# A two-layer attention encoder on one core: first weights through ScalarE's queue, norm factors beside x, and a first step ordered by product

## The chip, the core and the metric

The kernel runs on one core of one Trainium2 chip. The core has a matrix engine (TensorE, in the profile "PE" for its matmuls and "PEld" for its weight loads), three engines for elementwise work (VectorE "DVE", ScalarE "ACT", GpSimd "POOL") and a queue for transfers (SyncE, "SP"); ScalarE can issue transfers too ("ACTq" in the profile). Each engine works through its own list in order, and the lists are tied together by semaphores. Times are device microseconds of whole executions; the verdict rests on the median over runs. The measurement of the kernel before gave 853.75, 854.29 and 854.53 us, with a median of 854.29 us.

## The reference: what is computed

The input x has 512 tokens of 1024 values (float32). Two layers follow each other:

```
for i in range(DEPTH):                      # DEPTH = 2
    hn = rms_norm(x, norm_gain[i])
    if i % 2 == 0:  y = mixer_a(hn, ...)    # dilated windows, 3 groups, T5 bias
    else:           y = mixer_b(hn, ...)    # 2-D neighbourhood on an 8 x 64 grid
    x = x + y
```

Both mixers project hn with one wide weight matrix into queries, keys, values and a gate, norm queries and keys per head (with a gain per head dimension), add a learned bias to the scores, take a softmax, weigh the values, multiply by silu(gate) and project back to 1024. There are 16 heads of 64. In `rms_norm` each of the 1024 features has its factor in `norm_gain`; the division by the root of the mean square is per token.

## The kernel before

**Products in three parts.** Every float32 operand a is kept as a rounded part a_h (type float32r) and a rest a_l = a - a_h. A product is then three matmuls into one PSUM bank: a_h b_h, a_h b_l, a_l b_h (`mm3`). For weights, `split` makes the pair: ScalarE copies the raw weights to `wh` with rounding (L127), and VectorE or GpSimd subtracts (L131, `wl`; two of five go to GpSimd). For the normed input, `norm` makes `hn_h` on ScalarE (L379, x times the factor of its feature) and `hn_l` on VectorE (L380).

**Staging.** x lies transposed in SBUF as eight tiles of 128 features by 512 tokens (`x_all[:, k, :]`). Work goes over pairs of heads (hc, eight per layer). A projection (`project`) takes eight steps k, one per feature tile; in each step four token tiles i take three matmuls each, with `hn` as the stationary and `w` as the moving operand, into four PSUM accumulators. So a step has twelve matmuls. The division by the root of the mean square is applied later, when the accumulators are read, because the mean square of layer one is known only after all of x has been seen.

**Generators.** `loads`, `raws`, `splits` and `steps` (L157 to L196) hand the weights on in order. `raws` keeps three buffers `wraw` of 1024 columns in flight, each filled through SP's queue; the first is filled in two halves (L172 and L175), and one x load goes between them. `behind` holds three more x loads (tiles 2-3, 4-5, 6-7), one of which follows each later weights load. `splits` works up to four roundings ahead.

**What sets the order.** PE's order is written out by hand: `run` walks `main` (the projections) and lets `side` (norms, transposes, scores and so on) in between, by a planner's clock that adds a price per matmul. `project` yields after each token tile, and at each yield `pump` lets `side` go on when its due time is reached; `project` may also name a stamp that must be there first (`need`, here "na": norm k+1 must be written before step k of the first projection). The order on ACT, DVE, POOL and SP is laid out by the framework from a simulated timeline, except for instructions pinned with `keep_in_program_order`.

**The start.** SP loads x tile 0 (`load_x`, L343), the first half of the first weights (L172), x tile 1 and so on. ACT's queue loads `ng`, the 2 x 8 norm factors per partition (L349), and `hg`, the head gains (L363), from which four one-column VectorE instructions make `gk` (L366). Nine matmuls on a constant (`busy`, L358) keep PE occupied until data is there. `side` begins with the eight `norm` calls, each followed by the square of the tile before (L383, ScalarE) and later by the sums (L1146, VectorE).

Of the kernel before, what the change touches and what calls it, by code (L numbers as in the profile page):

```python
# [13 lines left out]
F32 = mybir.dt.float32  # L14
# [3 lines left out]
ALU = mybir.AluOpType  # L18
# [4 lines left out]
P = 128  # L23
S = 512
# [3 lines left out]
KT = 8  # L28
EPS = 1e-6
SCALE = DH ** -0.5  # L30
# [12 lines left out]
def tile_hybrid_encoder(  # L43
# [2 lines left out]
    xt: bass.AP,  # L46
    xg: bass.AP,
    w: bass.AP,
    norm_gain: bass.AP,
    head_gain: bass.AP,  # L50
    t5t: bass.AP,
    rpb: bass.AP,
# [4 lines left out]
    nc = tc.nc  # L57
# [3 lines left out]
    big = ctx.enter_context(tc.tile_pool(name="big", bufs=1))  # L61
# [21 lines left out]
    def bank(name):  # L83

        return ps_side.tile([P, 512], F32, tag="side", name=name)
# [13 lines left out]

    hn_h = big.tile([P, KT, S], F32R, name="hn_h")  # L100
    hn_l = big.tile([P, KT, S], F32R, name="hn_l")
    x_all = big.tile([P, KT, S], F32, tag="y", name="x_all")
    y_l = big.tile([P, KT, S], F32R, name="y_l")

    def rsqrt(eng, r, ss, n, scale):
# [16 lines left out]
    turn, pool = [0], [2, 5]  # L122

    def split(raw, n):
        h = wp.tile([P, 512], F32R, tag="wh", name="wh", bufs=4)[:, :n]
        l = wp.tile([P, 512], F32R, tag="wl", name="wl", bufs=4)[:, :n]
        nc.scalar.copy(h, raw)  # L127
        turn[0] += 1
        to_pool = turn[0] * pool[0] % pool[1] < pool[0]
        eng = nc.gpsimd if to_pool else nc.vector  # L130
        eng.tensor_sub(l, raw, h.bitcast(F32))  # L131
        return h, l
# [24 lines left out]
    def loads():  # L157
        for off, n, ks in blocks():
            per = 1024 // n
            for k in range(0, ks, per):  # L160
                m = min(per, ks - k)
                yield w[:, off + k * n : off + (k + m) * n], m * n, n
# [3 lines left out]
    def raws():  # L166
        queue = []
        for src, cols, n in loads():
            raw = wp.tile([P, 1024], F32, tag="wraw", name="wraw", bufs=3)
            dst = raw[:, :cols]  # L170
            if not begun:
                nc.sync.dma_start(dst[:, :n], src[:, :n])  # L172
                begun.append(load_x(1, 2))
                dst, src = dst[:, n:], src[:, n:]
            nc.sync.dma_start(dst, src)  # L175
            if behind:
                behind.pop()()
            queue.append((raw, cols, n))
            if len(queue) > 2:
                yield queue.pop(0)  # L180
        yield from queue
# [55 lines left out]
    def chore(now):  # L237

        if now and chores and next(chores[0], "end") == "end":
            chores.pop(0)  # L240

    def project(stat_h, stat_l, n, evac, guard, need=None):

        acc = {i: ps_acc.tile([P, 512], F32, tag="acc", name="acc") for i in range(4)}
        for k in range(KT):
            chore(1 <= k < KT - 2)
            if need:
                yield need, min(k + 1, KT - 1)
            if k == KT - 1:
                yield guard  # L250
            h, l = next(wsteps)
            for i in range(4):
                mm3(acc[i][:, :n], stat_h(k, i), stat_l(k, i), h, l, k == 0, k == KT - 1)
                if k == KT - 1:
                    evac(i, acc[i])
                yield
# [69 lines left out]
    ng = cp.tile([P, 2, KT], F32, name="ng")  # L326
# [13 lines left out]
        rsqrt(nc.vector, rs_n, ssq, 4, 1.0 / D)  # L340

    def load_x(k0, k1):
        nc.sync.dma_start(x_all[:, k0:k1, :], xt[:, k0:k1, :])  # L343

    warm = cp.tile([P, 1], F32, name="warm")
    nc.vector.memset(warm, 0.0)
    nc.scalar.activation(warm, warm, AF.Exp)
    load_x(0, 1)
    nc.scalar.dma_start(ng, norm_gain)  # L349
    behind += [  # L350
        lambda: load_x(6, KT),
        lambda: load_x(4, 6),
        lambda: load_x(2, 4),
    ]
    busy = bank("busy")
    for _ in range(9):
        wide = lambda n: ones[:, 0:1].to_broadcast([P, n])
        nc.tensor.matmul(busy, wide(P), wide(S), start=True, stop=True)  # L358
    wsteps = steps()
    wsteps = chain([next(wsteps)], wsteps)  # L360

    hg = cp.tile([P, 8], F32, name="hg")
    nc.scalar.dma_start(hg, head_gain)  # L363
    gk = cp.tile([P, 4], F32, name="gk")
    for i, (a, b) in enumerate(((0, 3), (1, 4), (2, 5), (6, 7))):
        nc.vector.scalar_tensor_tensor(  # L366
            gk[:, i : i + 1], hg[:, a : a + 1], -SCALE, hg[:, b : b + 1], op0=ALU.mult, op1=ALU.mult
        )

    def scales_a():  # L370
        pa = spread()
# [2 lines left out]

    def norm(layer, k, xk):

        g = ng[:, layer, k : k + 1]
        h, l = hn_h[:, k, :], hn_l[:, k, :]
        nc.scalar.activation(h, xk, AF.Copy, scale=g)  # L379
        return nc.vector.scalar_tensor_tensor(l, xk, g, h.bitcast(F32), op0=ALU.mult, op1=ALU.subtract)  # L380
# [755 lines left out]
    def side():  # L1136
        for k in range(KT):
            norm(0, k, x_all[:, k, :])
            if k:
                square_a(k - 1)  # L1140
            stamp["na", k] = 0
            yield 1000
        square_a(KT - 1)
        for k in range(1, KT):
            yield 1300
            nc.vector.tensor_add(x_all[:, 0, :], x_all[:, 0, :], x_all[:, k, :])  # L1146
        yield 1500
        row_scale(row_sums(x_all[:, 0, :]))
        st["y_h"] = big.tile([P, KT, S], F32R, tag="y", name="y_h")
        yield 2500  # L1150
        bias_lines()
        st["e", 0] = bias_a(0)
        yield 2500
        scales_a()
        first_out()
        stamp["rs", "a"] = 0
        for hc in range(NHC):
            if hc < NHC - 1:
                yield from k_a(hc)
                yield from chain(q_a(hc), v_a(hc))  # L1160
                if moved(hc):
                    yield from st.pop(("land", hc))
                yield from attn_a(hc)
                if hc == 1:
                    bias_rows()
            else:
                gap[0] = cycle((500, 500, 700))
                yield from chain(q_a(hc), k_a(hc))
                yield from attn_a(hc)
        yield from residual(xg)  # L1170
        stamp["ya", KT - 1, "y"] = 0
        yield "wait", ("x", KT - 1), 800
        for f in range(KT):
            square_b(f)
            yield 600
        yield 2600
        row_scale(row_sums(st.pop("ssq")))
        stamp["rs", "b"] = 0
        yield 5000
        nc.scalar.mul(rs_half, spread(), 0.5)  # L1180
        stamp["rs", "all"] = 0
        for hc in range(NHC):
            yield from side_b(hc)
        yield from residual(xm_d)
        stamp["yb", KT - 1, "y"] = 0

    run(main(), side())


# [27 lines left out]
def _layout(x, norm_gain, a_w_in, a_w_out, a_q_gain, a_k_gain, t5_bias,  # L1217
            b_w_in, b_w_out, b_q_gain, b_k_gain, b_rpb):
    f = lambda a: np.asarray(a)
    x, norm_gain, t5_bias = f(x), f(norm_gain), f(t5_bias)  # L1220
    wa, wao = f(a_w_in)[0].reshape(KT, P, -1), f(a_w_out)[0].reshape(KT, P, D)
    wb, wbo = f(b_w_in)[0].reshape(KT, P, -1), f(b_w_out)[0].reshape(KT, P, D)

    def outs(w):
        k = KT - 1
        blk = (w[:k, :, :512], w[:k, :, 512:896], w[k:, :, :512], w[k:, :, 512:896], w[:, :, 896:])
        return [b.transpose(1, 0, 2).reshape(P, -1) for b in blk]

    def cols(w, starts):
        blk = np.concatenate([w[:, :, s : s + P] for s in starts], axis=2)  # L1230
        return blk.transpose(1, 0, 2).reshape(P, -1)

    parts = []
    for hc in range(NHC):
        c = lambda g, i: (3 * g + i) * D + P * hc
        parts.append(cols(wa, [c(1, 1), c(2, 1), c(1, 2), c(2, 2)]))
        parts.append(cols(wa, [c(0, 0), c(1, 0), c(2, 0), c(0, 1)]))
        parts.append(cols(wa, [c(0, 2)]))
        parts.append(cols(wa, [9 * D + P * hc]))
    parts += outs(wao)  # L1240
    for hc in range(NHC):
        parts.append(cols(wb, [i * D + P * hc for i in range(3)]))
        parts.append(cols(wb, [3 * D + P * hc]))
    parts += outs(wbo)
    w = np.concatenate(parts, axis=1)

    hg = np.concatenate([f(a_q_gain)[0], f(a_k_gain)[0], f(b_q_gain), f(b_k_gain)]).T
    hg = np.concatenate([hg, hg])
    rt = f(b_rpb)[0].transpose(0, 2, 1)
    rpb = np.stack([rt[:, :, 7 - r + _GRID_ROWS] for r in _GRID_ROWS], axis=1).reshape(P, 248)  # L1250
    oh, mask = _constants()
    norm_gain = norm_gain.reshape(2, KT, P).transpose(2, 0, 1)
    xt = x[0].reshape(P, 4, KT, P).transpose(3, 2, 1, 0).reshape(P, KT, S)
    xg = x[0].reshape(8, 64, KT, P)[_GRID_ROWS].transpose(3, 2, 1, 0).reshape(P, KT, S)
    return [xt, xg, w, norm_gain, hg, t5_bias.T, rpb, oh, mask]


_NAMES = ["xt", "xg", "w", "norm_gain", "head_gain", "t5t", "rpb", "onehot", "maskc"]


# [17 lines left out]
```

## Time and profile before

| | |
|---|---|
| median of 3 runs | 854.29 us (853.75 to 854.53) |
| the profiled execution | 854.65 us, span 852.7 us |
| PE busy | 843.6 us (99% of the span), 5547 matmuls |
| PE weight loads busy | 702.7 us (82%) |
| DVE / ACT / POOL busy | 520.2 / 431.3 / 307.1 us |
| moved by the transfers | 141.23 MB, mean 166 GB/s |

The profiled execution lies 0.36 us above the median of the runs. Its span begins with the first instruction and ends with the last; 1.95 us of its time lie outside the span. The rows of a timeline give the start (us), the length (us), engine, line, operation, output and inputs; "xN" with a length covers N instructions that follow each other. In brackets stands how long the engine had been idle and what released it. PE's rows overlap: the distance between two starts tells the rate, not their lengths. The chain of waits follows the work that ended last back to its start, and prints it in order of time.

### The profile page before, as it was taken

How to read it: one execution, taken by the hardware profiler on the slowest of the kernel's cores; microseconds unless marked ns; L12 is line 12 of the kernel's file. 1: busy time of each engine (PE TensorE's matmuls, PEld its weight loads, DVE VectorE, ACT ScalarE, POOL GpSimd, SP SyncE). 2: the span in 40 equal slices, each digit the busy share in tenths (PEclk: the TensorE clock that was granted, in tenths of full speed). 3: DMA queues.
4: the chain of work that ended last, by engine and by line, in shares of the span. 5: the costliest groups of instructions: out<-in, count | busy, mean ns of one | idle time of the engine just before them, and what ended most of it. 6: DMA issues, size and time to landing. Idle time of an engine off the chain costs nothing.

```text
span 852.7 us, 15400 instructions
## 1 busy us (share of the span) xinstructions
PE 843.6 (99%) x5547; PEld 702.7 (82%) x5547; DVE 520.2 (61%) x1335; ACT 431.3 (51%) x924; POOL 307.1 (36%) x493
## 2 busy tenths in 40 slices
PE   8999999999999999999999999999999999999998
PEld 6788878788788788788788787789998898889786
DVE  6445684674675675675675745447567656766642
ACT  7433653653652652652653554355366655665531
POOL 2252541542542542542531341121344335542411
PEclk9999999999999999999999999999999999999999
DMA  7346277477478378378375562174245654555223
GB/s 250 111 130 208 87 226 219 153 222 227 137 230 241 105 239 240 98 238 238 96 247 153 147 190 78 60 244 142 82 142 150 168 162 149 170 163 160 99 98 126
DMA packets 65372, 141.23 MB, mean 166 GB/s; under 512 B 5904, under 2 KB 23248, under 8 KB 65296
## 3 DMA queue, kind: packets, MB, share of 16 engines
q1 hardware_dynamic: 65008, 140.24, 53.7%
q8 instruction: 44, 0.72, 0.4%
q14 instruction: 32, 0.26, 0.1%
q10 hardware_dynamic: 288, 0.01, 0.0%
HBM read 109.11 MB, written 31.12 MB: 164 GB/s over the span
## 4 chain that ended last, share of the span: by engine, by line
PE 87%; ACT 4%; DMA 4%; DVE 3%; issue 1%; POOL 1%; SPq 0%; ACTq 0%; POOLq 0%; DVEq 0%
PE acc L206 74%; PE log L206 5%; PE o L206 5%; PE tp L210 3%; DMA qd<-rawq 1%; ACT p L655 1%; ACT p L814 1%; DMA rp<-in_rpb 1%; ACT p L1067 1%; DMA qt<-qd 1%; POOL sq L270 1%; ACT wh L127 1%; DMA hg<-in_head_gain 0%; DVE wl L131 0%; DMA eb<-lb_d 0%
## 5 line engine op out<-in xcount | busy, mean ns | idle before, releaser
L127 ACT CAST wh<-wraw 128x512 fp32r<-128x512 f32 (+1 forms) x276 | 162.0, 588 | 291.4 <-PE acc L206 251.0
L206 PE MATMUL acc<-wh,hn_h 128*128 128x512 f32 (+1 forms) x768 | 294.2, 383 | 1.7 <-ACT wh L127 0.9
L206 PE MATMUL acc<-wh,hn_l 128*128 128x512 f32 (+1 forms) x768 | 286.3, 373 | 0.0
L206 PE MATMUL acc<-wl,hn_h 128*128 128x512 f32 (+1 forms) x768 | 285.8, 372 | 0.4 <-DVE wl L131 0.4
L131 POOL TENSOR_TENSOR wl<-wraw,wh 128x512 fp32r<-128x512 f32 (+1 forms) x110 | 137.0, 1245 | 359.4 <-ACT wh L127 320.0
L131 DVE TENSOR_TENSOR wl<-wraw,wh 128x512 fp32r<-128x512 f32 (+1 forms) x166 | 111.1, 670 | 135.8 <-ACT wh L127 131.5
L206 PEld LDWEIGHTS acc<-wh,hn_h 128*128 128x128 f32 x768 | 144.6, 188 | 29.3 <-issue 4.9
L206 PEld LDWEIGHTS acc<-wh,hn_l 128*128 128x128 f32 x768 | 144.4, 188 | 20.8
L206 PEld LDWEIGHTS acc<-wl,hn_h 128*128 128x128 f32 x768 | 144.8, 189 | 19.8 <-DVE wl L131 0.9
L206 PE MATMUL acc<-hn_h,wh 128*128 128x512 f32 x192 | 77.0, 401 | 0.9 <-ACT rawq L460 0.6
L206 PE MATMUL acc<-hn_h,wl 128*128 128x512 f32 x192 | 74.9, 390 | 0.0
L206 PE MATMUL acc<-hn_l,wh 128*128 128x512 f32 x192 | 74.8, 390 | 0.0
L655 ACT ACTIVATE p<-p,mn 128x512 f32<-128x512 f32 (+3 forms) x128 | 69.3, 586 | 0.0
L814 ACT ACTIVATE p<-p,mn 128x512 f32<-128x512 f32 (+1 forms) x64 | 44.8, 701 | 45.0 <-DVE mn L803 44.1
L273 DVE TENSOR_REDUCE ss<-sq 128x4 f32<-128x256 f32 (+1 forms) x96 | 48.4, 504 | 30.7 <-POOL sq L272 19.7
L727 DVE STREAM_TRANSPOSE tr<-p 128x512 f32<-128x512 f32 (+1 forms) x80 | 53.7, 682 | 9.9 <-ACT p L655 9.5
L272 POOL TENSOR_TENSOR sq<-rawk 128x256 f32<-128x256 f32 x64 | 40.5, 639 | 52.7 <-ACT rawk L460 44.9
L206 PE MATMUL acc<-y_h,wh 128*128 128x512 f32 x128 | 52.1, 407 | 0.0
L206 PE MATMUL acc<-y_h,wl 128*128 128x512 f32 x128 | 50.0, 391 | 0.0
L206 PE MATMUL acc<-y_l,wh 128*128 128x512 f32 x128 | 49.9, 390 | 0.0
L206 PEld LDWEIGHTS acc<-hn_h,wh 128*128 128x128 f32 x192 | 36.1, 188 | 10.8 <-ACT rawk L460 2.1
L206 PEld LDWEIGHTS acc<-hn_h,wl 128*128 128x128 f32 x192 | 36.0, 188 | 7.7
(138 smaller groups left out, 1087.0 us busy)
## 6 DMA issues: line engine op xcount, KB each, us to landing
wraw<-in_w SPq DMA_DIRECT2D x95, 512.0 KB
wraw<-in_w SPq DMA_DIRECT2D x38, 384.0 KB
td<-tr SPq DMA_DIRECT2D x14, 1024.0 KB
pt<-td SPq DMA_DIRECT2D x56, 256.0 KB
qd<-rawq SPq DMA_DIRECT2D x6, 1024.0 KB
qt<-qd SPq DMA_DIRECT2D x24, 256.0 KB
td<-tr SPq DMA_DIRECT2D x6, 896.0 KB
pt<-td SPq DMA_DIRECT2D x24, 224.0 KB
```

What stands on the lines that cost most here:

```text
L127: nc.scalar.copy(h, raw)
L131: eng.tensor_sub(l, raw, h.bitcast(F32))
L206: nc.tensor.matmul(o, l, r, **kw)
L210: nc.tensor.transpose(o, i, ident)
L270: nc.gpsimd.tensor_mul(sq.rearrange("p (f a r) -> p a f r", f=4, a=4), v, v)
L272: nc.gpsimd.tensor_mul(sq, v, v)
L273: nc.vector.tensor_reduce(ss[:, i * ns : (i + 1) * ns], sq.rearrange("p (a b) -> p a b", b=64), axis=AX.X, op=ALU.add)
L655: nc.scalar.activation(pr, pr, AF.Copy, scale=mn[:, 3:4])
L727: nc.vector.transpose(dst, src[:, :n].rearrange("p (i b k) -> p i b k", b=4, k=32))
L814: nc.scalar.activation(row, row, AF.Exp, bias=mn[:, 1:2], scale=-1.0, accum_out=mn[:, 2:3])
L1067: nc.scalar.activation(pr[:, o : o + n], pr[:, o : o + n], AF.Exp, bias=mn[:, 0:1], scale=-1.0, accum_out=mn[:, 2:3])
```

## The change

The change has four parts.

1. The norm factors no longer have a tensor and a transfer of their own. The host puts them in front of x (16 columns per partition), and the load of x tile 0 brings them along. `norm` of layer one reads them from there; for layer two GpSimd copies them to `ng`.
2. The first half of the first weights is issued on ScalarE's queue instead of SP's, and its rounded part is made by VectorE (`tensor_copy`) instead of ScalarE.
3. The load of `hg` and the four `gk` instructions move into a function `gains`, called by `side` at norm 4; the load goes through SP, and the four instructions are pinned in program order.
4. In step k = 0 of the first projection the twelve matmuls go by product (four of hn_h wh, four of hn_h wl, four of hn_l wh) with one yield at the end. There are eight instead of nine `busy` matmuls.

```diff
+    x_ng = big.tile([P, 2 * KT + KT * S], F32, tag="y", name="x_all")
+    x_all = x_ng[:, 2 * KT :].rearrange("p (k t) -> p k t", k=KT)
...
-        nc.scalar.copy(h, raw)
+        if turn[0]:
+            nc.scalar.copy(h, raw)
+        else:
+            nc.vector.tensor_copy(h, raw)
...
-                nc.sync.dma_start(dst[:, :n], src[:, :n])
+                nc.scalar.dma_start(dst[:, :n], src[:, :n])
...
+            if need and k == 0:
+                for i in range(4):
+                    matmul(acc[i][:, :n], stat_h(k, i), h, start=True, stop=False)
+                for i in range(4):
+                    matmul(acc[i][:, :n], stat_h(k, i), l, start=False, stop=False)
+                for i in range(4):
+                    matmul(acc[i][:, :n], stat_l(k, i), h, start=False, stop=False)
+                yield
+                continue
...
-        nc.sync.dma_start(x_all[:, k0:k1, :], xt[:, k0:k1, :])
+        lo = 2 * KT + S * k0 if k0 else 0
+        hi = 2 * KT + S * k1
+        nc.sync.dma_start(x_ng[:, lo:hi], xt[:, lo:hi])
...
-    nc.scalar.dma_start(ng, norm_gain)
...
-    for _ in range(9):
+    for _ in range(8):
...
-    nc.scalar.dma_start(hg, head_gain)
...
+    def gains():
+        nc.sync.dma_start(hg, head_gain)
+        nc.gpsimd.tensor_copy(ng.rearrange("p l k -> p (l k)"), x_ng[:, : 2 * KT])
+        for i, (a, b) in enumerate(((0, 3), (1, 4), (2, 5), (6, 7))):
+            m = nc.vector.scalar_tensor_tensor(
+                gk[:, i : i + 1], hg[:, a : a + 1], -SCALE, hg[:, b : b + 1], op0=ALU.mult, op1=ALU.mult
+            )
+            tc.keep_in_program_order(m)
...
-        g = ng[:, layer, k : k + 1]
+        g = (ng if layer else x_ng[:, : 2 * KT].rearrange("p (l k) -> p l k", l=2))[:, layer, k : k + 1]
...
             stamp["na", k] = 0
+            if k == 4:
+                gains()
```

More of the change, by code (lines that the diff above doesn't have):

```diff
@@ L48, in tile_hybrid_encoder @@
     w: bass.AP,
-    norm_gain: bass.AP,
     head_gain: bass.AP,
@@ L101, in tile_hybrid_encoder @@
     hn_l = big.tile([P, KT, S], F32R, name="hn_l")
-    x_all = big.tile([P, KT, S], F32, tag="y", name="x_all")
+    x_ng = big.tile([P, 2 * KT + KT * S], F32, tag="y", name="x_all")
+    x_all = x_ng[:, 2 * KT :].rearrange("p (k t) -> p k t", k=KT)
     y_l = big.tile([P, KT, S], F32R, name="y_l")
@@ L362, in tile_hybrid_encoder @@
     hg = cp.tile([P, 8], F32, name="hg")
-    nc.scalar.dma_start(hg, head_gain)
     gk = cp.tile([P, 4], F32, name="gk")
[L365 to L368, printed above, removed]
+    def gains():
[6 more added lines that the diff above has]
+            tc.keep_in_program_order(m)
     def scales_a():
@@ L1251, in _layout @@
     oh, mask = _constants()
-    norm_gain = norm_gain.reshape(2, KT, P).transpose(2, 0, 1)
-    xt = x[0].reshape(P, 4, KT, P).transpose(3, 2, 1, 0).reshape(P, KT, S)
+    norm_gain = norm_gain.reshape(2, KT, P).transpose(2, 0, 1).reshape(P, 2 * KT)
+    xt = x[0].reshape(P, 4, KT, P).transpose(3, 2, 1, 0).reshape(P, KT * S)
+    xt = np.concatenate([norm_gain, xt], axis=1)
     xg = x[0].reshape(8, 64, KT, P)[_GRID_ROWS].transpose(3, 2, 1, 0).reshape(P, KT, S)
-    return [xt, xg, w, norm_gain, hg, t5_bias.T, rpb, oh, mask]
-_NAMES = ["xt", "xg", "w", "norm_gain", "head_gain", "t5t", "rpb", "onehot", "maskc"]
+    return [xt, xg, w, hg, t5_bias.T, rpb, oh, mask]
+_NAMES = ["xt", "xg", "w", "head_gain", "t5t", "rpb", "onehot", "maskc"]
 def kernel(**inputs):
```

## The prediction

> **What bounds the kernel now.** I read the page first, then PE's waits over the whole span, then the chain and the timelines of the first 15 us, because the change touches nothing later.
>
> ```profile
> span 852.7 us, 15400 instructions
> PE 843.6 (99%) x5547; PEld 702.7 (82%) x5547; DVE 520.2 (61%) x1335; ACT 431.3 (51%) x924; POOL 307.1 (36%) x493
> ```
>
> PE is the bound: 99% busy, and no other engine passes 61%.
>
> ```profile
> PE acc L206 <- ACT rawq L460: 1.4, 2, 0.8
> PE o L206 <- DMA eb<-lb_d: 0.9, 1, 0.9
> PE busy L358 <- DVE warm L346: 0.9, 1, 0.9
> PE acc L206 <- ACT wh L127: 0.9, 1, 0.9
> PE acc L206 <- DVE wl L131: 0.4, 1, 0.4
> PE tp L210 <- ACT p L655: 0.4, 1, 0.4
> ```
>
> These rows (us in total, times, longest) are all that PE waits for in 852.7 us. Rows three to five lie at the start, 2.2 us together; the other three make 2.7 us in some 840. So a change to the start can win only there: whatever brings the unbroken run of matmuls forward shortens the whole by that much, if the supply of operands follows.
>
> ```profile
> 1.23 4.26 DMA hg<-in_head_gain
> 5.51 0.07 DVE gk L366
> 5.88 0.14 DVE hn_l L380
> 6.46 0.70 DVE wl L131
> 7.20 2.88 PE acc L206 x6
> ```
>
> The chain (start, length): the tiny load of the head gains holds VectorE until 5.5; behind it stand `gk`, then `hn_l`, then the first `wl`, which PE needs for its second matmul.
>
> ```profile
> 0.92 4.21 PE L358 MATMUL busy<-ones 128*128 128x512 f32 x9 [0.92 <-DVE warm L346]
> 6.00 0.80 PE L206 MATMUL acc<-wh,hn_h 128*128 128x512 f32 x1 [0.88 <-ACT wh L127]
> 7.20 0.80 PE L206 MATMUL acc<-wl,hn_h 128*128 128x512 f32 x1 [0.40 <-DVE wl L131]
> 7.79 0.63 PE L206 MATMUL acc<-wh,hn_l 128*128 128x512 f32 x1
> 9.50 0.58 PE L206 MATMUL acc<-wh,hn_h 128*128 128x512 f32 x1
> 9.92 0.40 PE L206 MATMUL acc<-wl,hn_h 128*128 128x512 f32 x1
> 13.83 0.39 PE L206 MATMUL acc<-wh,hn_h 128*128 128x512 f32 x1
> 14.05 0.39 PE L206 MATMUL acc<-wl,hn_h 128*128 128x512 f32 x1
> ```
>
> Seven matmuls start before 9.92 (6.00, 7.20, and five from 7.79 to 9.50, (9.50 - 7.79) / 4 = 0.43 us apart). The eighth starts at 9.92 and the 25th, the first of step 2, at 13.83: 3.91 / 17 = 0.23 us apart. PE thus works at half rate until 9.92, 2.72 us after the dense run began at 7.20, and at full rate from there on. (The profile's column of granted clock says 1.00 in the half-rate stretches too, in the rows of the next fence; I go by the distances.)
>
> **The change part by part.** Rows of ACT's, SP's and VectorE's views; the two that begin with a stretch (2.00:3.00) give PE, PEld, DVE, ACT and POOL busy, then granted clock, share of the transfer engines and GB/s.
>
> ```profile
> 0.73 0.40 ACTq L349 DMA_DIRECT2D ng<-in_norm_gain  x1
> 3.66 0.72 ACT L379 ACTIVATE hn_h<-x_all,ng 128x512 fp32r<-128x512 f32 x1 [0.99 <-DMA ng<-in_norm_gain]
> 5.33 0.62 ACT L127 CAST wh<-wraw 128x512 fp32r<-128x512 f32 x1 [0.95 <-DMA wraw<-in_w]
> 0.74 0.38 SPq L343 DMA_DIRECT2D x_all<-in_xt  x1
> 1.18 0.41 SPq L172 DMA_DIRECT2D wraw<-in_w  x1
> 1.64 0.42 SPq L343 DMA_DIRECT2D x_all<-in_xt  x1
> 5.50 0.33 SPq L343 DMA_DIRECT2D x_all<-in_xt  x1
> 9.24 0.35 SPq L175 DMA_DIRECT2D wraw<-in_w  x1
> 13.12 0.35 SPq L175 DMA_DIRECT2D wraw<-in_w  x1
> 2.00:3.00 1.00, 1.00 (x4) 0.82 (x3) 0.00 (x0) 0.65 (x2) 0.00 (x0) 1.00 0.90 284
> 3.00:4.00 1.00, 1.00 (x3) 0.80 (x3) 0.00 (x0) 0.34 (x1) 0.00 (x0) 1.00 0.77 224
> L823 DVE COPY pt<-tp 128x512 f32<-128x512 f32 x8 | 5.5, 688 | 2.8 <-PE tp L210 2.7
> ```
>
> *First weights on ACT's queue.* They were issued at 1.18 and used at 5.33, 4.15 us later, after x tile 0 in the same queue. ACT's queue has its first slot at 0.73, where `ng` went. So they are usable between 3.66 (when `ng`, issued there, released its reader) and 0.73 + 4.15 = 4.88. I take 4.4: the slot gives 0.45, and another 0.45 I put on not standing behind x tile 0 and on the two small loads that are gone (the transfer engines are at 0.77 to 0.90 with only 224 to 284 GB/s while they run). Everything later on SP is issued one slot (1.64 - 1.18, about 0.45) earlier.
>
> *Norm factors with x.* x tile 0 grows by 16 of 512 columns, and now shares with the weights. Usable at 3.66 before; at most the 256 KB of the weights in front of it, 0.9 us at 284 GB/s. I take 3.9, so `hn_h` ends at 3.9 + 0.72 = 4.6. The copy to `ng` on POOL (16 columns) has nothing queued behind it before the first `wl` at 11.09 and is needed only in layer two: nothing.
>
> *Rounding on VectorE.* This trace has no copy of this kind from SBUF. The nearest row is the 128x512 copy from PSUM, 0.69 us; from below, a one-column `gk` instruction took 0.07 to 0.15. I take 0.69: `wh` is there at 5.1, and PE starts at about 5.15. ACT loses 0.62.
>
> *The `gk` instructions move.* VectorE is free from the start, so `wl` runs from 5.1 to 5.8 and `hn_l` from 5.8 to 6.55. The instructions' 0.37 us come again behind `hn_l` of tile 4.
>
> ```profile
> 14.36 2.45 DVE L380 SCALAR_TENSOR_TENSOR hn_l<-x_all,ng,hn_h 128x512 fp32r<-128x512 f32 x2
> 16.73 0.68 DVE L131 TENSOR_TENSOR wl<-wraw,wh 128x512 fp32r<-128x512 f32 x1
> 10.40 1.13 ACT L127 CAST wh<-wraw 128x512 fp32r<-128x512 f32 x2
> 11.09 1.40 POOL L131 TENSOR_TENSOR wl<-wraw,wh 128x512 fp32r<-128x512 f32 x1 [9.66 <-ACT wh L127]
> SPq L705 <- DVE mn L1057: 16.6, 6, 4.3
> ```
>
> What stands behind them there is the `wl` of step 5 (ends 17.41), which PE needs at 13.83 + 36 x 0.23 = 22.1: 4.7 us of cover, even with PE 2 us earlier 2.7. `hg` is issued on SP, where the weights load at 9.24 waits for its buffer and leaves room from 6.8; with the old flight of 4.26 us it lands by 11 to 14, ahead of its use. If it fell behind the next weights load (13.12), it would land at 17.8 and VectorE would stand for some 2 us, still inside the cover. I cost it at nothing. The x load at 5.50, which waited 0.7 us for `hg`, goes earlier.
>
> *The step by product.* From 5.15 four matmuls of 0.43 run to 6.87 before `wl` (5.8) is needed, four more to 8.6 before `hn_l` (6.55). The 0.4 us wait goes, and of the 1.2 us between PE's first two matmuls only 0.43 stay. One `busy` matmul less ends the occupation at about 4.7; nothing waits for it. The single yield moves the norms of `side` by up to a step of the planner; the nearest prices for what that could do later are the waits of 0.4 to 0.9 us above, in either direction; I take zero.
>
> *The sum.* Dense work from 5.15 instead of 7.20, full rate again 2.72 us after: 7.87. By 9.92 that makes 2.72 / 0.43 + (9.92 - 7.87) / 0.23 = 6.3 + 8.9 = 15.2 matmuls instead of 7, a lead of 8.2 x 0.23 = 1.9 us.
>
> *What is late next.* Step 2 takes its `wl` from POOL, which ended at 11.09 + 1.40 = 12.49; PE wanted it at 14.05. That caps the lead at 1.56 us, unless this `wl` moves too. It hangs on ACT's roundings at 10.40, ahead of which one rounding (0.62) is gone and the loads come 0.45 earlier. I move it by 0.45: cap 2.0, so 1.9 stands.
>
> From the profiled execution, 854.65 - 1.9 = 852.75. The median of the runs is 0.36 lower (852.4); since the runs may owe that 0.36 to a better start, I do not carry all of it: **852.5 us**. A difference below 0.2% of 854.29, 1.7 us, counts as none here.
>
> The Trainium skill (page "TensorE: Matmul & The Clock Gate", Part 1) says that the half rate is a gate that opens at the end of a busy, free-running window of about 3.4 us. By it the moment would not follow the first matmul but jump by whole windows, from 9.92 to about 6.5 or not at all; the trace agrees on the halved rate, and one trace cannot show the grid. The sum by it would be the first or the second of the rivals below.
>
> **The rivals.**
>
> *The rate doubles at 9.92 as before.* For it: the row shows one moment, and nothing says what sets it. Then 4.77 / 0.43 = 11.1 matmuls instead of 7: 4.1 x 0.23 = 0.94 us, 853.4. If VectorE takes `hn_l` ahead of the rounding, PE starts near 6.1 and full rate comes at 8.8: 11.1 matmuls again, and the same time.
>
> *The rate doubles sooner.* PE's pause shrinks from 0.88 + 0.4 to about 0.5 us, so the occupation may count. Full rate from 6.5 would give 3.1 + 14.9 = 18 matmuls, 2.5 us, but the supply at step 2 caps it at 2.0: 852.3.
>
> *The two queues only share.* For it: the transfer share is 0.77 to 0.90 already at 2 to 4 us. Then x tile 0 is 0.9 us late (`hn_h` ends at 5.3), the weights come at 4.88, PE starts at 5.6, full rate at 8.32: 6.3 + 7.0 = 13.3 matmuls, 1.45 us, 852.8. The Trainium skill (page "DMA: Bandwidth & Descriptors", section "Issuing engines are not separate DMA queues") says just this, that a second issuing engine saves only issue time. By that rule the gain is 1.45 of the 1.9; no run here shows it yet.
>
> *Slower: the lists after the start come out in another order.* ACT, DVE, POOL and SP are laid out from a timeline that now begins differently, with one load less and `side` moved by a step. The place is the bias load `eb` in layer two, where six issues on SP already waited 16.6 us together for VectorE, and for which PE waits 0.9 us once. If it came late for all six, PE would wait 5.4 us: 854.29 - 1.9 + 5.4 = 857.8. It decides from four such waits (3.6 us) on. Against it: PE's hand-written order is the same from step 1 on, and PE waits three times only in 840 us.
>
> **How the numbers follow.** Forecast 0.46, of which 0.36 with over 1.7 us; doubling at 9.92 or a late rounding 0.17; sooner 0.12; shared queues 0.13; slower 0.12. Faster by over 0.2%: 0.36 + 0.12 = 0.48; slower 0.12; the rest, 0.40, within. Range: below, the cheap rounding (0.54 us less) and 2.5 us without the cap, 851.8, rounded out to 851.5; above, 853.4 with one new wait of 0.9: 854.4.
>
> **What would show it.** Right: the weights issued at 0.73 by ACTq and rounded by DVE before 5.2; PE's first `acc` matmul near 5.15, no wait between the first twelve; starts 0.23 apart from about 7.9; PE's 25th matmul near 11.9; `gk` behind `hn_l` of tile 4, without a wait for `hg`; the same three waits afterwards. Wrong: the first `acc` matmul after 5.6, PE waiting for `wl` of step 2, starts 0.43 apart until 9.9, or new waits after 30 us.

## The result, and the profile after

The changed kernel takes 858.55 us (858.33 to 860.23, six runs) against 854.14 us (852.12 to 855.01, six runs): a ratio of 1.0061, with an interval of 1.005 to 1.0072. It is slower by about 4.4 us, where 852.5 us was forecast. Its profiled execution has these lines on the page:

```profile
span 856.8 us, 15397 instructions
PE 849.2 (99%) x5546; PEld 700.8 (82%) x5546; DVE 517.8 (60%) x1336; ACT 430.9 (50%) x923; POOL 311.8 (36%) x494
```

PE is busy for 5.6 us longer than the 843.6 us of before, with one matmul less. Its waits over the whole span (us in total, times, longest) are these:

```profile
PE acc L209 <- ACT rawq L477: 1.3, 2, 0.7
PE busy L371 <- DVE warm L360: 0.9, 1, 0.9
PE acc L209 <- ACT hn_h L396: 0.6, 1, 0.6
PE tp L213 <- ACT p L672: 0.4, 1, 0.4
PE o L209 <- DVE ss L285: 0.3, 1, 0.3
PE acc L209 <- ACT rawk L477: 0.2, 1, 0.2
```

They sum to 3.7 us, against 4.9 before (the rows in the prediction). So no wait explains the loss: PE waits less and still ends later. The timeline of PE shows the start and the end:

```profile
5.27 1.18 PE L209 MATMUL acc<-wh,hn_h 128*128 128x512 f32 x4 [0.57 <-ACT hn_h L396]
6.29 1.08 PE L209 MATMUL acc<-wl,hn_h 128*128 128x512 f32 x4
7.21 1.08 PE L209 MATMUL acc<-wh,hn_l 128*128 128x512 f32 x4
...
10.88 0.39 PE L209 MATMUL acc<-wh,hn_h 128*128 128x512 f32 x1
11.11 0.50 PE L209 MATMUL acc<-wl,hn_h 128*128 128x512 f32 x1
852.64 0.39 PE L209 MATMUL acc<-y_h,wl 128*128 128x512 f32 x1
```

The first matmul on data comes at 5.27 instead of 6.00, and the 25th at 10.88 instead of 13.83: the kernel is 2.95 us ahead there. But its last one starts at 852.64, where that of before has this row:

```profile
848.49 0.39 PE L206 MATMUL acc<-y_h,wl 128*128 128x512 f32 x1
```

It is 4.15 us behind at the end. Between the 25th and the last matmul 7.1 us were lost, though the waits there are shorter (2.2 us against 2.7). The chain of waits shows how; these are two stretches of 99 matmuls from the chain of before (start, length):

```profile
243.82 22.48 PE acc L206 x99
307.94 22.48 PE acc L206 x99
```

And the like stretches from the chain of the changed kernel:

```profile
243.06 23.06 PE acc L209 x99
307.96 23.06 PE acc L209 x99
```

The same 99 matmuls take 23.06 us instead of 22.48: 0.233 us instead of 0.227 for one. The instructions, their shapes and their order in these stretches are the same in both. The groups of instructions, kept apart by shape (busy us, mean ns, idle before), show it for the projections in which hn is the moving operand. Before:

```profile
L206 PE MATMUL acc<-hn_h,wh 128*128 128x512 f32 x192 | 77.0, 401 | 0.9 <-ACT rawq L460 0.6
L206 PE MATMUL acc<-hn_h,wl 128*128 128x512 f32 x192 | 74.9, 390 | 0.0
L206 PE MATMUL acc<-hn_l,wh 128*128 128x512 f32 x192 | 74.8, 390 | 0.0
```

After:

```profile
L209 PE MATMUL acc<-hn_h,wh 128*128 128x512 f32 x192 | 78.0, 406 | 0.9 <-ACT rawq L477 0.6 <-ACT rawk L477 0.2
L209 PE MATMUL acc<-hn_l,wh 128*128 128x512 f32 x192 | 75.8, 395 | 0.0
L209 PE MATMUL acc<-hn_h,wl 128*128 128x512 f32 x192 | 75.8, 395 | 0.0
```

In these groups the mean matmul is 5 ns longer. In the output projections it is 7 ns longer for two products (y_h wh from 407 to 414, y_l wh from 390 to 397) and 1 ns for the third; in the projections in which w is the moving operand, with 512 columns, it is 1 to 2 ns longer (401 to 402, 391 to 392 and 393), taken over the whole kernel. What differs for all of them is where their operands lie. The pool `big` holds hn_h, hn_l, the x tile and y_l in this order, and the pool with wh and wl comes behind it. The x tile grew by 16 columns, 64 bytes per partition, so y_l, wh and wl moved by 64 bytes, while hn_h, hn_l and y_h (which later takes the x tile's place) stayed. Before, by the sizes of the tiles in the code, the starts of all of these differed by multiples of 2048 bytes.

### The profile page after: what moved, and what is told of

Read it like the earlier page. It is cut to its first block, busy times and chain, and to the rows that moved or that the text cites. A ratio compares the mean times of both kernels' runs of the same rounds, so it can differ in the third digit from the quotient of the medians.

```text
span 856.8 us, 15397 instructions
## 1 busy us (share of the span) xinstructions
PE 849.2 (99%) x5546; PEld 700.8 (82%) x5546; DVE 517.8 (60%) x1336; ACT 430.9 (50%) x923; POOL 311.8 (36%) x494
## 4 chain that ended last, share of the span: by engine, by line
PE 95%; ACT 3%; DVE 1%; DMA 0%; issue 0%; POOL 0%; ACTq 0%
PE acc L209 81%; PE log L209 5%; PE o L209 5%; PE tp L213 3%; ACT p L1084 1%; ACT p L672 1%; ACT p L831 0%; DMA x_all<-in_xt 0%; ACT wh L128 0%; ACT rawk L477 0%; PE pa L209 0%; PE pl L209 0%; DVE p L820 0%; PE pk L209 0%; DVE p L1074 0%
## 5 line engine op out<-in xcount | busy, mean ns | idle before, releaser
L134 POOL TENSOR_TENSOR wl<-wraw,wh 128x512 fp32r<-128x512 f32 (+1 forms) x110 | 139.0, 1263 | 361.5 <-ACT wh L128 330.3
```

## The experiments

Theory A: TensorE's operands moved against each other, and that slows its matmuls. Theory B: the start changed the order in which ACT, DVE, POOL and SP are laid out, and this costs the time.

**The displacement alone.** The kernel before, with an x tile that is longer but not fuller; shown for 64 bytes, and with 8 and 32 columns for 32 and 128 bytes:

```diff
-    x_all = big.tile([P, KT, S], F32, tag="y", name="x_all")
+    x_all = big.tile([P, KT * S + 16], F32, tag="y", name="x_all")[:, : KT * S].rearrange("p (k t) -> p k t", k=KT)
```

> The kernel before, with x's tile 16 columns (64 bytes) longer and nothing in them: every tile allocated behind it, among them y_l, wh and wl, lies 64 bytes further from hn_h, hn_l and y_h than before, and every engine has the same instructions in the same order as before. Theory A (the changed kernel loses pace because TensorE's operands moved 64 bytes against each other): it won 2.95 us by its 25th matmul and lies 4.15 us behind at its last, so the displacement costs 7.1 us: 861.2 us, with 0.233 us instead of 0.227 between the matmuls that have hn as moving operand. Theory B (the other order of the lists on the engines costs the time): no change, 854.1 us.

> As the 64-byte displacement of the kernel before, with 128 bytes. Theory A: slower than 854.1, by an amount that it does not give; if only the place within 128 bytes counts, no change, 854.1. Theory B: 854.1.

> As the 64-byte displacement of the kernel before, with 32 bytes. Theory A: between 854.1 and 861.2 if the cost grows with the distance, or as much as with 64 bytes if any displacement breaks the alignment. Theory B: 854.1.

Measured, against 853.84 us for the kernel before on the same chip: 861.77 us with 64 bytes (ratio 1.0091, interval 1.0076 to 1.0106), 864.18 us with 128 (1.012, 1.0105 to 1.0135), 866.74 us with 32 (1.0149, 1.0133 to 1.0164). In the three profiles the instructions of all five engines follow each other as in before, by line, operation and tile name, to the last one. From the chain with 64 bytes:

```profile
246.30 23.06 PE acc L206 x99
```

And with 32 bytes:

```profile
248.64 23.09 PE acc L206 x99
```

Theory B falls: with no instruction moved, 64 empty bytes bring the stretches of 23.06 us and cost 7.9 us (861.77 us, where theory A expected 861.2). The cost does not grow with the distance: 32 bytes cost most, more than either reading of theory A expected.

**The change with its operands kept together.** The x tile goes to the front of the pool and y_h takes its last 4096 columns, so that all of them move by the same 64 bytes:

```diff
+    x_ng = big.tile([P, 2 * KT + KT * S], F32, tag="y", name="x_all")
     hn_h = big.tile([P, KT, S], F32R, name="hn_h")
     hn_l = big.tile([P, KT, S], F32R, name="hn_l")
-    x_ng = big.tile([P, 2 * KT + KT * S], F32, tag="y", name="x_all")
...
-        st["y_h"] = big.tile([P, KT, S], F32R, tag="y", name="y_h")
+        y_ng = big.tile([P, 2 * KT + KT * S], F32R, tag="y", name="y_h")
+        st["y_h"] = y_ng[:, 2 * KT :].rearrange("p (k t) -> p k t", k=KT)
```

> The changed kernel with its x tile allocated ahead of hn_h and hn_l and y_h placed behind the 16 columns, so that hn, y_h, y_l, wh and wl are all displaced by the same 64 bytes; the engines' lists stay those of the changed kernel. Theory A: the old pace and the won start, about 851.2 us (854.1 - 2.95), 0.227 us between matmuls. Theory B: 858.5 us as the changed kernel.

Measured: 852.13 us against 853.84 (ratio 0.9978, 0.9968 to 0.9989), 0.9 us more than the 851.2 that theory A expected. The stretches in its chain are back at the old length:

```profile
242.59 22.50 PE acc L209 x99
```

This version beats both kernels. With the same instructions as the changed kernel on every engine, the place of two tiles decides between 0.61% slower and 0.22% faster.

**Which operands, and which distance.** Three more placements of the kernel before. First, the 64 bytes behind y_l, so that only wh and wl move (and the tiles behind them, which the projections don't read):

```diff
-    y_l = big.tile([P, KT, S], F32R, name="y_l")
+    y_l = big.tile([P, KT * S + 16], F32R, name="y_l")[:, : KT * S].rearrange("p (k t) -> p k t", k=KT)
```

> The kernel before with the 64 empty bytes behind y_l instead of in front of it: hn, y_h and y_l keep their places, wh and wl (and all behind them) are 64 bytes further; the engines' lists are the same. If what counts is the distance between the weights and the operand that TensorE reads beside them, it costs at least what the displacement of y_l, wh and wl together cost (861.8, 7.9 us over before), and the output projection's matmuls on y_l, whose weights had moved along with y_l there, are slowed now as those on y_h are. If the place of y_l was the cause, no change: 854.

Measured: 861.72 us against 854.15 (1.0094, 1.0078 to 1.0109), as much as with y_l displaced too. So the place of y_l is not needed for the loss; the weights against hn and y are enough.

Second, 256 bytes, by two small tiles that change places:

```diff
-    ng = cp.tile([P, 2, KT], F32, name="ng")
+    ng = mid.tile([P, 2, KT], F32, name="ng")
...
-        t5 = cp.tile([32, 48], F32, name="t5")
+        t5 = mid.tile([32, 48], F32, name="t5")
```

(`mid` is a new pool between `big` and that of the weights.)

> The kernel before with two small tiles (ng, t5, 256 bytes together) allocated behind y_l instead of ahead of hn: hn, y_h and y_l lie 256 bytes lower, wh and wl stay. If the distance counts only within 256 bytes, no change: 854. If any distance that is not a multiple of 512 bytes is slow, 862 to 867, as with 32, 64 and 128 bytes. Matmuls 0.227 us apart in the first case, 0.229 to 0.235 in the second.

Measured: 854.33 us against 854.15 (1.0004, 0.9994 to 1.0014), no difference. From its chain:

```profile
244.08 22.48 PE acc L206 x99
```

Third, hn_l alone is put 64 bytes off, by the same two small tiles around it:

```diff
+    ng = big.tile([P, 2, KT], F32, name="ng")
     hn_l = big.tile([P, KT, S], F32R, name="hn_l")
+    t5 = big.tile([32, 48], F32, name="t5")
```

> The kernel before with two small tiles allocated around hn_l (64 and 192 bytes that lay ahead of hn), so that hn_l alone lies 64 bytes off the others within 256 bytes; hn_h is 256 bytes lower, which cost nothing with both, and the engines' work is the same. Only one of the three matmuls of a product uses hn_l. If what counts is the distance between the two operands of one matmul, a third of the projections' loss comes back: of the 5.7 us that the projections lost with all weights 64 bytes off (the rest was the output projections' 2.0), 1.9 us: 856.0, and the output projections keep their old pace. If it is any mixture of places among TensorE's operands, as much as with all weights: 859 or more. If only the weights' place counts: 854.1.

Measured: 861.83 us against 854.22 (1.0095, 1.0075 to 1.0115). A stretch of its chain, and the group of matmuls on hn_h and wl:

```profile
247.21 22.91 PE acc L206 x99
...
L206 PE MATMUL acc<-hn_h,wl 128*128 128x512 f32 x192 | 75.7, 395 | 0.0
```

One operand out of place costs as much as the weights did, though only one matmul of three uses it. The second row bears on the reason: hn_h and wl lie as they lay in the run with 256 bytes, and yet their matmul takes 395 ns instead of 390. The output projections, which don't read hn, keep their old pace (407, 391 and 390 ns). So it is not simply the distance between the two operands of one matmul, each for itself; what the matmuls beside it read counts too. That their reads overlap is the likely reason, but which two reads get in each other's way is not settled by these runs. What they bear out, for the distances tried, is the rule of thumb that all operands of a stream of matmuls should start at the same place within 256 bytes.

**The start, part by part.** Since the kernel with its operands together keeps the won start, each part was taken back from it, one at a time. The steps' old order:

```diff
-            if need and k == 0:
+            if False:
```

> The changed kernel with all operands displaced together (852.1), but step 0 in the old order, token tile by token tile. PE's second matmul then waits for wl (the rounding's end plus 0.69 us) and the third for hn_l (0.71 more). Theory S (the order by product hides these waits): the first matmuls pause some 0.9 us, PE's 25th comes 0.5 to 0.9 us later than at 10.9, time 852.7 to 853.0. Rival (the start is bound by the supply of later steps, not by step 0): 852.1, and the pause is made up by step 2.

Measured: 852.14 us against 854.15 (0.9986, 0.9977 to 0.9996). PE's rows:

```profile
5.46 0.50 PE L209 MATMUL acc<-wh,hn_h 128*128 128x512 f32 x1 [0.76 <-ACT hn_h L396]
6.06 0.51 PE L209 MATMUL acc<-wl,hn_h 128*128 128x512 f32 x1
6.72 0.50 PE L209 MATMUL acc<-wh,hn_l 128*128 128x512 f32 x1 [0.16 <-DVE hn_l L397]
```

The waits are there as expected, some 0.8 us over the first three starts (5.46 to 6.72, less two matmuls at 0.23). The time does not decide between the two sides: its interval overlaps with that of all four parts (0.9968 to 0.9989).

The head gains at the start again, their instructions unpinned:

```diff
-    def gains():
-        nc.sync.dma_start(hg, head_gain)
+    nc.scalar.dma_start(hg, head_gain)
...
-            tc.keep_in_program_order(m)
```

(The copy to `ng` stays at norm 4.)

> The changed kernel with all operands displaced together (852.1), but the head gains loaded at the start on ScalarE's queue, and their four VectorE instructions free in order, as before the change. They now stand behind the first wl and ahead of hn_l of tile 0, which step 0 needs only for its last four matmuls, 8 x 0.23 to 8 x 0.43 us after the first. Theory S (late gains are what matters): VectorE waits for the load to about 5.5 and hn_l comes after 6.6; no PE wait if it is there by 7.1: 852.1 to 852.6. Rival (this load was the whole loss of the old start): back to 854.

Measured: 852.71 us against 854.15 (0.9986, 0.9977 to 0.9995). The rival, back to 854, falls. VectorE reaches the gains behind the first `wl`, when their load is there, and does not wait:

```profile
5.91 0.36 DVE L380 SCALAR_TENSOR_TENSOR gk<-hg 128x1 f32<-128x1 f32 x4
```

The other way round, only the late gains in the kernel before:

```diff
+    def gains():
+        nc.sync.dma_start(hg, head_gain)
...
+            if k == 4:
+                gains()
```

> The kernel before, places of the tiles unchanged, with only the third part of the change: the head gains loaded through SP at norm 4 and their four VectorE instructions pinned there. hn_l is then ready by 5.2 and wl follows ScalarE's rounding at 5.95 to 6.65 instead of 7.15, so PE's second matmul starts near 6.7 instead of 7.2. If the load of the gains was the loss that the chain of before names: 0.5 us won, 853.6. If the first weights were what the start waited for: PE's first matmul stays at 6.0 and the 25th gains under 0.3 us, 853.9 to 854.1.

Measured: 853.83 us against 854.21 (0.9993, 0.9984 to 1.0003), which cannot be told from no change. From PE's first matmul to its second it took 0.73 us instead of 1.20. But this execution ran at full rate and that of before at half rate, so the matmul itself accounts for 0.23 instead of 0.43 us of it; the pause shrank from 0.77 to 0.50 us:

```profile
5.72 0.50 PE L206 MATMUL acc<-wh,hn_h 128*128 128x512 f32 x1 [0.60 <-ACT wh L127]
6.45 0.50 PE L206 MATMUL acc<-wl,hn_h 128*128 128x512 f32 x1 [0.23 <-DVE wl L131]
```

The first rounding on ScalarE again:

```diff
-        if turn[0]:
-            nc.scalar.copy(h, raw)
-        else:
-            nc.vector.tensor_copy(h, raw)
+        nc.scalar.copy(h, raw)
```

> The changed kernel with all operands displaced together (852.1), but ScalarE rounds the first weights again. Its list then has the rounding (0.62) ahead of hn_h (0.72), one after the other from about 4.7: PE starts at 6.05 instead of 5.3 to 5.45, 0.6 to 0.75 us later: 852.7 to 852.9. Rival (the supply of step 2 bounds the start): 852.1.

Measured: 853.24 us against 854.21 (0.9989, 0.9979 to 1.0). PE starts at 6.16 instead of 5.33, a little later than the 0.6 to 0.75 us that were expected, since ScalarE does both:

```profile
4.87 0.62 ACT L127 CAST wh<-wraw 128x512 fp32r<-128x512 f32 x1 [2.21 <-DMA wraw<-in_w]
5.39 1.34 ACT L393 ACTIVATE hn_h<-x_all 128x512 fp32r<-128x512 f32 x2
6.16 1.19 PE L206 MATMUL acc<-wh,hn_h 128*128 128x512 f32 x4 [1.46 <-ACT hn_h L393]
```

The first weights on SP's queue again:

```diff
-                nc.scalar.dma_start(dst[:, :n], src[:, :n])
+                nc.sync.dma_start(dst[:, :n], src[:, :n])
```

> The changed kernel with all operands displaced together (852.1), but the first weights are issued on SP again, at 1.18 behind x tile 0. If ACT's queue brings them forward (my 4.4 against 5.33): PE starts some 0.4 us later or more, 852.5 to 852.9. Rival (the two queues only share the transfer engines, x tile 0 becoming later by as much): PE starts no later than 5.4, 852.1 or a little less.

Measured: 852.95 us against 854.21 (0.9985, 0.9975 to 0.9996).

```profile
3.59 0.72 ACT L396 ACTIVATE hn_h<-x_all 128x512 fp32r<-128x512 f32 x1 [1.36 <-DMA x_all<-in_xt]
5.03 0.43 DVE L130 CAST wh<-wraw 128x512 fp32r<-128x512 f32 x1 [4.13 <-DMA wraw<-in_w]
5.60 1.16 PE L209 MATMUL acc<-wh,hn_h 128*128 128x512 f32 x4 [0.90 <-DVE wh L130]
```

Without the second queue x is used at 3.59 and the weights at 5.03, and PE starts at 5.60, 0.27 us later than with all parts and between what the two sides expected.

The intervals of the four variants and of the kernel with all parts overlap, so the times don't rank the parts; the ratios (0.9985 to 0.9989 with a part taken back, 0.9978 with all) would give each 0.6 to 0.9 us, which the intervals don't show. The profiled executions tell more, if those are compared in which PE ran at the same rate. At full rate from the start, PE's 25th matmul came at 10.88 in the changed kernel. With the old order of the steps, with the rounding on ScalarE and with the weights on SP's queue, also at full rate, it came at:

```profile
11.84 0.39 PE L209 MATMUL acc<-wh,hn_h 128*128 128x512 f32 x1
11.74 0.39 PE L206 MATMUL acc<-wh,hn_h 128*128 128x512 f32 x1
11.44 0.39 PE L209 MATMUL acc<-wh,hn_h 128*128 128x512 f32 x1
```

These are 0.96, 0.86 and 0.56 us later. So the pause of the old order is not made up by step 2, against the rival. With the gains at the start it came at 13.00, against 13.06 with all parts, both at half rate until some 9.8: in this start the place of the gains is worth nothing that these rows show. Each of these numbers is one execution, and how much of them is left at the end is not shown. The parts together, with the operands in place, are worth 1.7 us (853.84 less 852.13).

## Why the prediction was wrong, and where it was right

**The step that failed** is the premise that the change "touches nothing later" than the first 15 us, with the count of what the 16 columns do: "x tile 0 grows by 16 of 512 columns, and now shares with the weights". I counted the columns as bytes to transfer. They are also bytes in SBUF, in front of y_l and the weights, and the displacement slows every projection until the end. By the trace it cost 7.1 us after the 25th matmul; alone it cost 7.9. Nothing in the profile of before shows an address. It could have been read from the code, as the tile stands ahead of y_l in its pool, but the price of it stands in no row.

**The slower rival** had the right sign for a wrong reason. It put new waits on the bias loads `eb` in layer two; the waits after are shorter than before (3.7 us against 4.9), and with 64 empty bytes the loss came without any change of order. (It also counted three waits in the last 840 us; the three rows hold four, as `rawq` has two.)

**The sum of the start met its number partly by luck.** With the operands together, 852.13 us was measured where 852.5 was forecast. But the ten executions behind it lie at 851.18 to 851.48 (five) and at 852.79 to 853.90 (five), with the median in the gap between them, and neither of the two leads seen at the 25th matmul (0.77 and 2.95 us, below) is the 1.9 of the sum. Its steps, against these rows of the changed kernel:

```profile
4.50 1.47 ACT L396 ACTIVATE hn_h<-x_all 128x512 fp32r<-128x512 f32 x2 [1.84 <-DMA x_all<-in_xt]
4.68 0.43 DVE L130 CAST wh<-wraw 128x512 fp32r<-128x512 f32 x1 [3.79 <-DMA wraw<-in_w]
9.65 1.40 POOL L134 TENSOR_TENSOR wl<-wraw,wh 128x512 fp32r<-128x512 f32 x1 [4.93 <-ACT wh L128]
15.30 0.35 DVE L382 SCALAR_TENSOR_TENSOR gk<-hg 128x1 f32<-128x1 f32 x4
```

- The weights were usable at 4.68 where I took 4.4, and x at 4.50 where I took 3.9. So the two queues mostly share, as the rival said: with the weights back on SP, x was there at 3.59 and the weights at 5.03, so that 0.35 us of the weights were bought with 0.9 us of x. (The four executions with both queues and the rounding on VectorE had x at 4.50 to 4.68 and the weights at 4.68 to 4.85. With SP's queue alone there is one such execution, so what the weights gained is less sure than what x lost.) The Trainium skill's rule (page "DMA: Bandwidth & Descriptors", section "Issuing engines are not separate DMA queues"), that a second issuing engine saves issue time only, agrees with that.
- The rounding on VectorE took 0.43 us, not 0.69. So `wh` was there at 5.11, near the 5.1 of the sum, by two errors that cancel; PE's start at 5.27 (5.15 forecast) is set by `hn_h`, which the sum had ready at 4.6.
- The gains came behind `hn_l` of tile 4 without a wait, at 15.30, as costed.
- The supply at step 2 was the term furthest off: the `wl` of POOL, which I moved forward by 0.45 us to a cap of 2.0, ended at 11.05 (9.65 + 1.40) instead of 12.49, 1.44 us earlier. PE took it at 11.11 with hardly a pause, so this cap did not bind at 2.0.
- The moment of the doubled rate was my weakest term. In the changed kernel's profiled execution full rate was there at the first matmul (four from 5.27 to 6.29 are 0.26 each); with the operands together it came late, as these rows of PE's timeline show (7.20 to 8.90 for four matmuls is 0.43 each, from 10.30 on 0.23):

```profile
5.33 2.07 PE L209 MATMUL acc<-wh,hn_h 128*128 128x512 f32 x4 [0.62 <-ACT hn_h L396]
7.20 1.91 PE L209 MATMUL acc<-wl,hn_h 128*128 128x512 f32 x4
8.90 1.56 PE L209 MATMUL acc<-wh,hn_l 128*128 128x512 f32 x4
10.30 0.40 PE L209 MATMUL acc<-wh,hn_h 128*128 128x512 f32 x1
13.06 0.39 PE L209 MATMUL acc<-wh,hn_h 128*128 128x512 f32 x1
```

That execution was 0.77 us ahead of before at the 25th matmul, near the 0.94 of the rival in which the rate doubles at 9.92; the changed kernel's own was 2.95 ahead. Both have the same list of instructions on PE and nearly the same start (5.27 and 5.33). So the moment belongs to the execution rather than to the kernel, and my 2.72 us after the start of dense work was a reading of one case.

## What to carry to other kernels

When a change makes a tile longer, look up which tiles are allocated behind it, and keep the float32r operands that TensorE reads in one stream at the same place within 256 bytes. If a kernel bound by PE gets slower without a new wait, compare stretches of the chain with the same count of matmuls before looking for a cause in the order of work. A part that changes both a schedule and a layout is best tried as an empty displacement first: it takes one line and leaves every instruction as it was.

## What the runs showed of the hardware

The pace of float32r matmuls with 512 columns depends on where their operands lie against each other: in the stretches shown 0.227 us with all at the same place within 256 bytes, 0.231 to 0.233 (22.91 and 23.06 to 23.09 us for 99) with some of them 32, 64 or 128 bytes off. Over this kernel that is 7.6 to 12.9 us (861.72 less 854.15, 866.74 less 853.84), 0.9% to 1.5%. The longer time shows in the matmuls' own durations, not in waits.

The granted clock changed in steps of equal length where the profile recorded it falling back. In the execution with 256 bytes the stretches are these (start and end, length, then PE, PEld, DVE, ACT, POOL busy, granted clock, transfer share, GB/s):

```profile
4.66:8.07 3.41, 1.35 (x5) 0.67 (x4) 1.64 (x6) 1.79 (x4) 0.00 (x0) 1.00 0.99 353
8.07:11.48 3.41, 3.41 (x9) 2.64 (x8) 3.21 (x5) 3.10 (x7) 0.07 (x1) 0.50 1.02 418
11.48:15.00 3.52, 3.52 (x17) 2.87 (x16) 3.19 (x5) 3.48 (x7) 1.61 (x2) 1.00 0.87 289
```

Full rate, half rate and full rate again follow each other 3.41 us apart: PE was busy for only 1.35 us of the first stretch, and the second ran at half rate although PE was busy throughout. The execution with hn_l alone shows the same steps, at 4.77, 8.18 and 11.59. This agrees with the windows of about 3.4 us that the Trainium skill names (page "TensorE: Matmul & The Clock Gate", Part 1). Such steps would account for the same start being 0.8 us ahead in one execution and 2.95 in another; no run here held the moment of the rate fixed, so that stays an argument.
